# First shift's products of three quarters moved to VectorE, with one ring of eight weight buffers for the first stage

## The chip, the cores and the metric

The kernel runs on one core of a Trainium2 chip. The metric is the device time of one execution in microseconds (us). Times inside an execution come from one profiled execution and count from the start of its span. TensorE is called PE, VectorE DVE, ScalarE ACT, GpSimd POOL; DMA transfers are issued from SyncE's queue (SP).

## The reference

One transformer block on 256 tokens of width 2048, all in FP32. Its first stage is the modulation and the big input product:

```python
mod = (silu(c) @ w_ada[l] + b_ada[l])[:, None, :]
sh1, sc1, g1, sh2, sc2, g2 = split(mod, 6)
u = layer_norm(x) * (1.0 + sc1) + sh1
mix = token_mixer(u, w_in[l], ...)      # u @ w_in, sliding-window attention, gated delta rule, projections
x = layer_norm(alpha * x + g1 * mix, ...)
u = layer_norm(x) * (1.0 + sc2) + sh2
x = layer_norm(alpha * x + g2 * hier_moe(u, ...), ...)   # 32 experts, two per token
```

`sh1` and `sc1`, the first shift and the first scale, are needed before any column of `u` exists: each is a vector of 2048 numbers, and each number is a dot product of `silu(c)` with a column of 2048 weights. So 32 MB of weights are read to make them.

## The kernel before

**The first stage (0 to about 195 us).** `u` is cut into four quarters of 512 columns (four slices of 128 in `xT`, transposed). For a quarter, `first_mods` makes 512 numbers of the scale and 512 of the shift; then the quarter of `u` can be formed and multiplied. The weights of one such 512-vector are four tiles `w` of 128x2048 (1 MB each). PE takes a tile in four column-tiled matmuls into `fa` (L192, `fa<-w,crep`, named `fa` + 1 for scale or 0 for shift + quarter); after four tiles ACT copies `fa` to `fr` (L199), PE transposes it in four pieces into `fc` (L169), and DVE reduces it to the column vector (L170) and adds the bias (L171). After the shift of a quarter come, four times, DVE's modulation of an `xT` slice (L175), ACT's cast `uh` (L176, the high part of `u`) and DVE's `ul` (L177, the low part).

**The input product of a quarter.** `quarter(q)` takes five weight tiles `w_kq`, each in two half jobs: ten jobs of a quarter. A job splits its 128x1024 half tile into `wh` (ACT cast, L275) and `wl = w - wh` (DVE, L276) and then runs 24 matmuls 128x256 into PSUM `wq`: eight times the three products `uh,wh` (L280), `ul,wh` (L281), `uh,wl` (L282). Names are `wq` + quarter + tile + half. The result is copied to `a0` or `szT` by ACT in quarter 0 (L334) and added to it by DVE in quarters 1 to 3 (L336). There are three buffers for `wh`, two for `wl` and two for `wq`.

**What sets the order.** `run` writes the jobs of a quarter down and puts a step of the next quarter's modulation between them, at the pace `QCH` in steps per job: the jobs of quarter 0 run beside the modulation of quarter 1, and so on; steps left over are written after the tenth job. The order of each engine's instructions in the finished program is then set by the framework's scheduler from this code; every engine works through its own list in that order. Tiles are loaded into a pool `wp` of four buffers, the first four into two larger areas (`early_room`), all in the order in which the SP queue lists them.

**Behind it** (195 to about 400 us) the remaining columns of `u @ w_in`, the attention, the gated delta rule and the projections run, again as three matmuls for a product; the four later modulation vectors are made there on DVE (L220, 128 operations `acc<-w,csil,acc`). From about 960 us the experts' weights stream through PE.

```python
QCH = 0.73
for _ in range(8 - FM + (LT[0] >= 0)):
    next(mods)
for q in range(4):
    quarter(q, dsts)
for q in range(3):
    run(few(mods, 8), QCH, split_at=2 * TQ)
```

Of the kernel before, what the change touches and what calls it, by code (L numbers as in the profile page):

```python
# [9 lines left out]
F32 = mybir.dt.float32  # L10
# [6 lines left out]
P = 128  # L17
D = 2048
KT = D // P
S = 256  # L20
NT = S // P
# [13 lines left out]
AHEAD = ((1, 1), (1, 3), (2, 1), (2, 3), (3, 1))  # L35
LATE = 0
TQ = 5
QCH = 0.73
FM = 2
LT = (-1, 0)  # L40
GS = (2, 6, 10)
NW2 = 6
PER = (1.66, 1.55, 0.85, 2.0)
# [23 lines left out]
def tile_block(ctx: ExitStack, tc: tile.TileContext, A: dict, out: bass.AP, dbg=None, upto=99):  # L67
    nc = tc.nc
    V, SC, G, T = nc.vector, nc.scalar, nc.gpsimd, nc.tensor
    MUL, ADD, SUB = ALU.mult, ALU.add, ALU.subtract  # L70
# [4 lines left out]
    def wload(src):  # L75
        w = wp.tile([P, 2048], F32, tag="w", name="w")
        nc.sync.dma_start(w, src)
        return w
# [29 lines left out]
    ident, ones = C("ident"), C("ones")  # L108
# [21 lines left out]
    csil = rb.tile([P, KT], F32, name="csil")  # L130
    SC.activation(csil, craw[:, 0:KT], AF.Silu)
    crep = gd.tile([P, KT, 32], F32, name="crep")
# [9 lines left out]
    r2 = up.enter_context(tc.tile_pool(name="r2", bufs=1, side=R))  # L142
# [3 lines left out]
    def pg(nm):  # L146
        return ps_g.tile([P, 512], F32, tag="g", name=nm)
# [9 lines left out]
    def early_room():  # L157

        a = r1.tile([P, 1024 + 7 * 512], F32, tag="G1", name="wx0")
        b = r2.tile([P, KT, S], F32, tag="X1", name="wx1").rearrange("p k s -> p (k s)")  # L160
        return [t[:, 2048 * j:2048 * j + 2048] for t in (a, b) for j in range(2)]

    def first_mods():

        def use(i, q, mr):
            dst = (sh1c, sc1c)[i][:, 4 * q:4 * q + 4]
            p = pg(f"fc{i}{q}")
            for m in range(4):
                T.transpose(p[:, m * P:(m + 1) * P], mr[:, m * P:(m + 1) * P], ident)  # L169
            V.tensor_reduce(dst, p.rearrange("p (m j r) -> p m j r", m=4, j=4)[:, :, :, 0], axis=AX.X, op=ADD)  # L170
            V.scalar_tensor_tensor(dst, dst, float(i), craw[:, KT * (i + 1) + 4 * q:KT * (i + 1) + 4 * q + 4],  # L171
                                   op0=ADD, op1=ADD)
            if i == 0:
                for k in range(4 * q, 4 * q + 4):
                    V.tensor_scalar(xT[:, k, :], xT[:, k, :], sc1c[:, k:k + 1], sh1c[:, k:k + 1], op0=MUL, op1=ADD)  # L175
                    SC.copy(uh[:, k, :], xT[:, k, :])  # L176
                    V.tensor_tensor(ul[:, k, :], xT[:, k, :], uh[:, k, :].bitcast(F32), op=SUB)  # L177

        late = []
        room = early_room()  # L180
        for q in range(4):
            for i in (1, 0):
                pa = pg(f"fa{i}{q}")
                for t in range(4):
                    src = A["w_a01"][(4 * i + q) * 4 + t]
                    if room:
                        w = room.pop(0)
                        nc.sync.dma_start(w, src)
                    else:
                        w = wload(src)  # L190
                    for k in range(4):
                        T.matmul(pa[32 * k:32 * k + 32, :], crep[:, 4 * t + k, :], w[:, 512 * k:512 * k + 512],  # L192
                                 start=(t == 0), stop=(t == 3))
                    if late and t == LT[1 - i]:
                        use(*late.pop())
                    if t < 3:
                        yield
                mr = rb.tile([P, 512], F32, tag="mr", name=f"fr{i}{q}")
                SC.copy(mr, pa)  # L199
                if i == 0 and LT[0] < 0:  # L200
                    use(i, q, mr)
                else:
                    late.append((i, q, mr))
                yield
        if late:
            use(*late.pop())
        yield

    mrs = {}

# [39 lines left out]
    uh = r2.tile([P, KT, S], F32R, name="uh")  # L250
    ul = r2.tile([P, KT, S], F32R, name="ul")
    sh1c = gd.tile([P, KT], F32, name="sh1c")
    sc1c = gd.tile([P, KT], F32, name="sc1c")
    xT = r1.tile([P, KT, S], F32, tag="M0", name="xT")
    xx = r2.tile([P, NT, D], F32, tag="X2", name="xx")
    nc.sync.dma_start(xx[:, 0, :], A["x"][0:P, :])
    nc.sync.dma_start(xx[:, 1, :], A["x"][P:2 * P, :])
    mods = first_mods()
    for _ in range(FM):
        next(mods)  # L260
    for t in range(NT):
# [3 lines left out]
        for kq in range(4):  # L265
            p = pg(f"xt{t}{kq}")
# [5 lines left out]
    def split(w, n=1024):  # L272
        h = r1.tile([P, n], F32R, tag="wh", name="wh", bufs=3)
        lo = r1.tile([P, n], F32R, tag="wl", name="wl", bufs=2)
        SC.copy(h, w)  # L275
        V.tensor_tensor(lo, w, h.bitcast(F32), op=SUB)  # L276
        return h, lo

    def mm3(p, a, b, first, last):
        T.matmul(p, a[0], b[0], start=first, stop=False)  # L280
        T.matmul(p, a[0], b[1], start=False, stop=False)  # L281
        T.matmul(p, a[1], b[0], start=False, stop=last)  # L282
# [29 lines left out]
    def quarter(q, dsts):  # L312

        for t in range(len(dsts) // 4):
            st = {}

            def prep(hf, t=t, st=st):
                if hf == 0:
                    st["w"] = wload(A["w_kq"][q * TQ + t])
                return split(st["w"][:, hf * 1024:(hf + 1) * 1024])  # L320

            def fin(sp, hf, t=t):
                h, lo = sp
                p = ps_w.tile([P, 512], F32, tag="ws", name=f"wq{q}{t}{hf}")
                for m in range(2):
                    for k in range(4):
                        kk = slice(k * 256 + m * P, k * 256 + m * P + P)
                        mm3(p[:, m * S:(m + 1) * S], (h[:, kk], lo[:, kk]), (uh[:, 4 * q + k, :], ul[:, 4 * q + k, :]),
                            k == 0, k == 3)
                        if k % 2 and m + k < 4:  # L330
                            yield
                dst = dsts[4 * t + 2 * hf].rearrange("p m s -> p (m s)")
                if q == 0:
                    SC.copy(dst, p)  # L334
                else:
                    V.tensor_tensor(dst, dst, p, op=ADD)  # L336

            for hf in range(2):
                jobs.append((lambda hf=hf, prep=prep: prep(hf), lambda sp, hf=hf, fin=fin: fin(sp, hf)))

    def first():
        if held.get("n") is None:
            held["n"] = jobs[0][0]()

    def run(chain=None, per=1.0, adas=0.0, steps=None, drain=True, split_at=None):

        c = a = 0.0
        first()
        todo = jobs[:split_at] if split_at else list(jobs)
        for i, (_, fin) in enumerate(todo):  # L350
            cur, held["n"] = held["n"], (jobs[i + 1][0]() if i + 1 < len(jobs) else None)
            sub = fin(cur)
            for _ in range(4):
                c += per / 4
                while chain is not None and c >= 1.0:
                    c -= next(chain, None) or 1.0
                a += adas / 4
                while a >= 1.0:
                    next(steps if steps is not None else ada, None)
                    a -= 1.0  # L360
                next(sub, None)
            for _ in sub:
                pass
        del jobs[:len(todo)]
        if drain and chain is not None:
            for _ in chain:
                pass
# [379 lines left out]
    def few(it, n):  # L747
        for _ in range(n):
            next(it, None)
            yield  # L750
# [7 lines left out]
        yield  # L758

    dsts = [a0[:, i:i + 2, :] for i in range(11)] + [None] + [szT[:, i:i + 2, :] for i in range(7)] + [None]  # L760
    for _ in range(8 - FM + (LT[0] >= 0)):
        next(mods)
    for q in range(4):
        quarter(q, dsts)
    for q in range(3):
        run(few(mods, 8), QCH, split_at=2 * TQ)
    for _ in mods:
        pass
    for dst, n in ((sml, "small"), (cmx, "cmx")):
# [215 lines left out]
    for c in range(4):  # L985
        cs = slice(c * 512, (c + 1) * 512)
        uq = rw.tile([P, 4, S], F32, tag="uq", name=f"uq{c}", bufs=2)
        for t in range(NT):
            V.scalar_tensor_tensor(x[t][:, cs], x[t][:, cs], mv[:, t, 0:1], l1[0][:, cs], op0=SUB, op1=MUL)
            V.scalar_tensor_tensor(x[t][:, cs], x[t][:, cs], rs[:, t], l1[1][:, cs], op0=MUL, op1=ADD)  # L990
            p = pg(f"ut{t}{c}")
# [46 lines left out]
    def pm(nm):  # L1038
        return ps_m.tile([P, 512], F32, tag="m", name=nm)
# [46 lines left out]
    for t in range(NT):  # L1086
        p = pm(f"rk{t}")
# [441 lines left out]
```

## Time and profile before

| | |
|---|---|
| median of three runs | 1835.93 us (1833.44 to 1836.46) |
| the profiled execution | 1836.7 us, of which the span is 1834.7 us |
| PE busy | 1742.0 us (95% of the span) |
| DVE busy | 906.3 us (49%) |
| ACT busy | 516.5 us (28%) |
| mean granted clock of PE | 0.987 of full speed |
| DMA | 628.58 MB, 343 GB/s over the span |

Busy shares are means over stages with different limits. "Idle before" in a row of the trace is the time in which that engine stood still ahead of the row, with what ended it. Rows with xN join N instructions of one kind that follow each other.

### The profile page before, as it was taken

To read this page: it belongs to the slowest core of one execution; us is meant where nothing else is said; L and a number is where in the kernel's file an instruction comes from. 1 tells how busy PE (TensorE), PEld (TensorE's weight loads), DVE (VectorE), ACT (ScalarE), POOL (GpSimd) and SP (SyncE) were. 2 spreads that over 40 slices of the span, in tenths; PEclk is the share of its full clock that TensorE was granted. 3 is DMA by queue.
4 is the path that set the end of the run, shared out by engine and by line. 5 is a ranking of instruction groups with operands and counts; after the bars stand their busy time and mean duration, and the time that the engine had idled before them with its cause. 6 is when DMAs were issued, how large, how long until landed. Compare 5 with 4: busy or idle time off the path is not lost. (4 is left out here: it accounts for less than half of the span.)

```text
span 1834.7 us, 27454 instructions
## 1 busy us (share of the span) xinstructions
PE 1742.0 (95%) x11514; PEld 1122.4 (61%) x11514; DVE 906.3 (49%) x1447; ACT 516.5 (28%) x956; POOL 42.1 (2%) x47
## 2 busy tenths in 40 slices
PE   5999999999999999998899999999999999999995
PEld 3778988898999999986444443444434444344341
DVE  3355898788878878668233222332223312232135
ACT  3333699336323444434211100111101110011101
POOL 1000000102000000000000000000000000000000
PEclk8999999999999999999999999999999999999998
DMA  8888566455877578878799999999999999999995
GB/s 356 320 320 312 211 245 225 174 207 200 300 266 269 205 284 325 345 303 354 319 383 420 420 420 421 420 421 420 421 420 420 420 421 420 420 420 421 401 422 232
DMA packets 87287, 628.58 MB, mean 343 GB/s; under 512 B 9828, under 2 KB 9828, under 8 KB 11252
## 3 DMA queue, kind: packets, MB, share of 16 engines
q1 hardware_dynamic: 86832, 626.43, 85.6%
q8 instruction: 92, 1.51, 0.3%
q10 hardware_dynamic: 328, 0.36, 0.1%
q14 instruction: 35, 0.29, 0.0%
HBM read 624.65 MB, written 2.10 MB: 342 GB/s over the span
## 5 line engine op out<-in xcount | busy, mean ns | idle before, releaser
L275 ACT CAST wh<-w 128x1024 fp32r<-128x1024 f32 x216 | 225.9, 1049 | 319.0 <-PE ws L281 114.1
L276 DVE TENSOR_TENSOR wl<-w,wh 128x1024 fp32r<-128x1024 f32 x216 | 264.8, 1226 | 81.0 <-PE mx L281 22.8
L1187 PE MATMUL pg<-w,XT 128*64 128x512 f32 x1024 | 277.9, 598 | 5.0 <-DMA w<-in_w_gu 2.8
L1187 PE MATMUL pu<-w,XT 128*64 128x512 f32 x1024 | 274.6, 592 | 0.0
L280 PE MATMUL ws<-uh,wh 128*128 128x256 f32 x896 | 261.2, 292 | 1.1 <-ACT wh L275 1.1
L282 PE MATMUL ws<-uh,wl 128*128 128x256 f32 x896 | 254.5, 284 | 4.4 <-DVE wl L276 3.9
L281 PE MATMUL ws<-ul,wh 128*128 128x256 f32 x896 | 253.7, 283 | 0.0
L1225 PE MATMUL pd<-w,hT 128*64 128x512 f32 x1016 | 234.1, 599 | 0.8 <-DVE hT L1202 0.8
L1194 DVE TENSOR_TENSOR hs<-hs,pu 128x512 f32<-128x512 f32 x16 | 11.0, 688 | 429.3 <-PE pu L1187 429.3
L280 PEld LDWEIGHTS ws<-uh,wh 128*128 128x128 f32 x896 | 169.8, 190 | 11.6 <-issue 7.5
L282 PEld LDWEIGHTS ws<-uh,wl 128*128 128x128 f32 x896 | 170.1, 190 | 8.6 <-DVE wl L276 7.1
L281 PEld LDWEIGHTS ws<-ul,wh 128*128 128x128 f32 x896 | 170.1, 190 | 0.5 <-issue 0.5
L220 DVE SCALAR_TENSOR_TENSOR acc<-w,csil,acc 128x1024 f32<-128x1024 f32 x128 | 164.3, 1300 | 10.6 <-DMA w<-in_w_ada 10.3
L1187 PEld LDWEIGHTS pu<-w,XT 128*64 128x64 f32 x1024 | 77.6, 137 | 146.2 <-issue 146.2
L1187 PEld LDWEIGHTS pg<-w,XT 128*64 128x64 f32 x1024 | 72.3, 136 | 135.5 <-issue 111.8
L1166 PEld LDWEIGHTS xg<-G,xh 128*128 128x128 f32 x1024 | 118.9, 191 | 41.2 <-issue 25.8
L1225 PEld LDWEIGHTS pd<-w,hT 128*64 128x64 f32 x1016 | 66.5, 136 | 124.0 <-issue 109.6
L1166 PE MATMUL xg<-G,xh 128*128 128x128 f32 x1024 | 130.5, 281 | 6.8 <-DVE x L1242 3.5
L1193 ACT ACTIVATE hs<-pg 128x512 f32<-128x512 f32 x16 | 9.6, 598 | 439.1 <-PE pg L1187 439.1
L370 ACT CAST dh<-pd 128x512 fp32r<-128x512 f32 x64 | 37.5, 586 | 281.3 <-DVE pd L1228 160.8
L1228 DVE SCALAR_TENSOR_TENSOR pd<-pd,wsl,g2b 128x512 f32<-128x512 f32 x64 | 48.5, 758 | 104.0 <-PE pd L1225 104.0
L280 PE MATMUL wq<-uh,wh 128*128 128x256 f32 x320 | 93.7, 296 | 5.1 <-ACT uh L176 2.7
(365 smaller groups left out, 2298.0 us busy)
## 6 DMA issues: line engine op xcount, KB each, us to landing
w<-in_w_gu SPq DMA_DIRECT2D x256, 1024.0 KB, 19.8
w<-in_w_dn SPq DMA_DIRECT2D x127, 1024.0 KB, 19.8
w<-in_w_ada SPq DMA_DIRECT2D x64, 1024.0 KB, 5.0
w<-in_w_in SPq DMA_DIRECT2D x56, 1024.0 KB, 5.0
w<-in_w_a SPq DMA_DIRECT2D x28, 1024.0 KB, 6.3
w<-in_w_kq SPq DMA_DIRECT2D x20, 1024.0 KB, 6.4
w<-in_w_pab SPq DMA_DIRECT2D x16, 1024.0 KB, 5.3
w<-in_w_out SPq DMA_DIRECT2D x16, 1024.0 KB, 6.0
```

The costliest lines, as they stand in the source:

```text
L220: V.scalar_tensor_tensor(acc[:, hc], w[:, hc], csil[:, k:k + 1], acc[:, hc], op0=MUL, op1=ADD)
L275: SC.copy(h, w)
L276: V.tensor_tensor(lo, w, h.bitcast(F32), op=SUB)
L280: T.matmul(p, a[0], b[0], start=first, stop=False)
L281: T.matmul(p, a[0], b[1], start=False, stop=False)
L282: T.matmul(p, a[1], b[0], start=False, stop=last)
L370: SC.copy(h, src)
L1166: T.matmul(p[:, k * P:(k + 1) * P], xh[t][:, (4 * kq + k) * P:(4 * kq + k + 1) * P], Gs[t].bitcast(F32), start=(t == 0), stop=(t == NT - 1))
L1187: T.matmul(dst[64 * e:64 * e + 64, :], XT[:, k, 64 * e:64 * e + 64], we[:, e * 1024 + hv * 512:e * 1024 + hv * 512 + 512], start=(k == 0), ...
L1194: V.tensor_tensor(hs, hs, pup, op=MUL)
L1225: T.matmul(pd[64 * e:64 * e + 64, :], hT[:, f, 64 * e:64 * e + 64], we[:, (2 * (f % 2) + e) * 512:(2 * (f % 2) + e + 1) * 512], start=(f = ...
L1228: V.scalar_tensor_tensor(pd, pd, ws, g2b[:, cs], op0=MUL, op1=MUL)
```

## The change

For quarters 1 to 3 the products of the shift leave PE. `beside` makes them on DVE: sixteen operations 128x512 for a quarter (one `tensor_scalar`, then fifteen `scalar_tensor_tensor`, L222 and L224 of the changed kernel), each adding a quarter of a weight tile times a column of `silu(c)` to one accumulator `acc`; then four matmuls with one column (`fs`, L230) sum it over the partitions, and DVE adds the bias (L231). The scale stays on PE (`on_pe`). Both halves of a quarter's modulation now run side by side in eleven steps instead of eight, and the pace `QCH` goes from 0.73 to 1.2. From quarter 1 on all loads of the stage, those of the jobs too, go round a ring of eight buffers (`wring`): two in a tile `ms` (which also holds the accumulator), two in `xs`, four from `wp`.

```diff
-QCH = 0.73
+QCH = 1.2
+    def wring(src):
+        w = ring[turn_of[0] % len(ring)]
+        turn_of[0] += 1
+        if w is None:
+            return wload(src)
+        nc.sync.dma_start(w, src)
+        return w
...
+        def beside(q, acc, got):
+            for t in range(4):
+                for k in range(4):
+                    wk, ck = got[t][:, 512 * k:512 * k + 512], csil[:, 4 * t + k:4 * t + k + 1]
+                    if t == k == 0:
+                        V.tensor_scalar(acc, wk, ck, None, op0=MUL)
                     else:
+                        V.scalar_tensor_tensor(acc, wk, ck, acc, op0=MUL, op1=ADD)
+                    if k % 2:
                         yield
+            dst, b = column(0, q)
+            p = pg(f"fs{q}")
+            for m in range(4):
+                T.matmul(p[:, m:m + 1], acc[:, m * P:(m + 1) * P], ones[:, 0:1], start=True, stop=True)
+            V.tensor_tensor(dst, p[:, 0:4], b, op=ADD)
+            yield
...
+        ring[:] = [ms[:, 512:512 + D], ms[:, 512 + D:512 + 2 * D], xs[:, 0:D], xs[:, D:2 * D]] + [None] * 4
...
+        for q in range(1, 4):
+            got = []
+            side, main = beside(q, ms[:, 0:512], got), on_pe(1, q)
+            for n in range(11):
+                if n >= 2:
+                    next(side, None)
+                if n % 2 == 0 and n < 8:
+                    got.append(load(0, q, n // 2))
+                if n % 2 and n < 8:
+                    next(main)
+                if n == 10:
+                    modulate(q)
                 yield
...
-                    st["w"] = wload(A["w_kq"][q * TQ + t])
+                    st["w"] = wring(A["w_kq"][q * TQ + t])
...
-    for _ in range(8 - FM + (LT[0] >= 0)):
+    for _ in range(9 - FM):
...
-        run(few(mods, 8), QCH, split_at=2 * TQ)
+        run(few(mods, 11), QCH, split_at=2 * TQ)
```

Elsewhere the lines only shift: `wh` is L322, `wl` L323, the three matmuls L327 to L329, the copy L381, the add L383, `uh` L190 in the changed kernel.

The order of the program moves at three places. First ACT, quarter 0, from the cast of the fourth job on: `wh` is a job's cast, `wq<quarter><tile><half>` a job's result that is copied. Before, then after:

```order
L275 CAST wh_338<-w_299 128x1024
L334 COPY a0_196<-wq000_273 128x512
L334 COPY a0_196<-wq001_305 128x512
L275 CAST wh_376<-w_374 128x1024
L334 COPY a0_196<-wq010_342 128x512
L275 CAST wh_406<-w_374 128x1024
L334 COPY a0_196<-wq011_380 128x512
L275 CAST wh_444<-w_442 128x1024
L334 COPY a0_196<-wq020_416 128x512
L275 CAST wh_482<-w_442 128x1024
```

```order
L322 CAST wh_338<-xs_264 128x1024
L381 COPY a0_196<-wq001_306 128x512
L381 COPY a0_196<-wq010_342 128x512
L381 COPY a0_196<-wq011_378 128x512
L322 CAST wh_374<-w_372 128x1024
L322 CAST wh_412<-w_372 128x1024
L381 COPY a0_196<-wq020_420 128x512
L381 COPY a0_196<-wq021_458 128x512
L322 CAST wh_447<-ms_263 128x1024
L322 CAST wh_487<-ms_263 128x1024
```

Before, a cast and a copy alternate, and the cast of job 5 stands ahead of the copy of job 3 (`wq011`). After, both casts of jobs 4 and 5 (`wh_374`, `wh_412`) stand behind the copies of jobs 2 and 3, and both casts of jobs 6 and 7 behind the copies of jobs 4 and 5.

Second ACT at the end of quarter 0, where quarter 1 of `u` is formed: `fr` is the copy of the last `fa`, `uh` the cast of the new quarter's slices. Before, then after:

```order
L275 CAST wh_596<-w_594 128x1024
L275 CAST wh_659<-w_594 128x1024
L334 COPY szT_197<-wq041_600 128x512
L199 COPY fr01_638<-fa01_505 128x512
L176 CAST uh_100<-xT_104 128x256
L275 CAST wh_691<-w_689 128x1024
L176 CAST uh_100<-xT_104 128x256 x3
```

```order
L381 COPY szT_197<-wq030_491 128x512
L381 COPY szT_197<-wq031_539 128x512
L213 COPY fr11_511<-fa11_319 128x512
L190 CAST uh_100<-xT_104 128x256
L322 CAST wh_535<-w_533 128x1024
L322 CAST wh_567<-w_533 128x1024
L190 CAST uh_100<-xT_104 128x256 x3
L322 CAST wh_601<-w_599 128x1024
```

Before, all ten jobs of quarter 0 are cast and run ahead of `fr`, and `wh_691`, behind the first `uh`, belongs to quarter 1. After, jobs 8 and 9 of quarter 0 (`wh_535`, `wh_567`, results `wq040`, `wq041`) stand behind `fr` and behind the first `uh`; PE's list has the same turn:

```order
L208 MATMUL fa11_319<-xs_264,crep_82 32x512 x4
L183 MATMUL fc11_513<-cst_61,fr11_511 128x128 x4
L230 MATMUL fs1_605<-cst_61,ms_263 128x1 x4
L327 MATMUL wq040_571<-uh_100,wh_535 128x256
L328 MATMUL wq040_571<-ul_101,wh_535 128x256
L327 MATMUL wq041_623<-uh_100,wh_567 128x256
L328 MATMUL wq041_623<-ul_101,wh_567 128x256
L329 MATMUL wq040_571<-uh_100,wl_536 128x256
```

So PE has the last scale tile, the transposes, the four summing matmuls and then at once job 8. The ends of quarters 1 and 2 read the same way.

Third DVE in the middle of quarter 1, from the add of job 3 (`wq111`) on; `wl` is a job's low part. Before, then after:

```order
L336 TENSOR_TENSOR a0_196<-a0_196,wq111_770 128x512
L276 TENSOR_TENSOR wl_797<-w_764,wh_796 128x1024
L336 TENSOR_TENSOR a0_196<-a0_196,wq120_806 128x512
L276 TENSOR_TENSOR wl_835<-w_832,wh_834 128x1024
L336 TENSOR_TENSOR a0_196<-a0_196,wq121_838 128x512
L276 TENSOR_TENSOR wl_873<-w_832,wh_872 128x1024
```

```order
L383 TENSOR_TENSOR a0_196<-a0_196,wq110_723 128x512
L224 SCALAR_TENSOR_TENSOR ms_263<-ms_263,csil_80 128x512 x2
L323 TENSOR_TENSOR wl_754<-xs_264,wh_753 128x1024
L383 TENSOR_TENSOR a0_196<-a0_196,wq111_757 128x512
L323 TENSOR_TENSOR wl_791<-xs_264,wh_790 128x1024
L383 TENSOR_TENSOR a0_196<-a0_196,wq120_798 128x512
L224 SCALAR_TENSOR_TENSOR ms_263<-w_796,csil_80,ms_263 128x512 x3
L383 TENSOR_TENSOR a0_196<-a0_196,wq121_838 128x512
L224 SCALAR_TENSOR_TENSOR ms_263<-w_796,csil_80,ms_263 128x512
L323 TENSOR_TENSOR wl_827<-w_824,wh_826 128x1024
L323 TENSOR_TENSOR wl_869<-w_824,wh_868 128x1024
```

Before, the `wl` of job j+2 follows the add of job j. After, two products stand between the add of job 2 (`wq110`) and the `wl` of job 4 (`wl_754`), and the `wl` of job 6 (`wl_827`) stands behind the add of job 5 (`wq121`), with a product between. Quarter 2 reads the same way.

## Rows read from the trace of the kernel before

**Rows 1.** The profile page: the span, the busy time of each engine, and the GB/s that the DMA moved in 40 equal slices of the span (four of them and a quarter are the first stage).

```profile
span 1834.7 us, 27454 instructions
PE 1742.0 (95%) x11514; PEld 1122.4 (61%) x11514; DVE 906.3 (49%) x1447; ACT 516.5 (28%) x956; POOL 42.1 (2%) x47
...
GB/s 356 320 320 312 211 245 225 174 207 200 300 266 269 205 284 325 345 303 354 319 383 420 420 420 421 420 421 420 421 420 420 420 421 420 420 420 421 401 422 232
```

**Rows 2.** A stretch of the first stage: length, then busy time and number of instructions of PE, PEld, DVE, ACT, POOL, then granted clock, DMA share and GB/s.

```profile
140.00:160.00 20.00, 20.00 (x165) 16.73 (x168) 9.51 (x13) 7.12 (x7) 0.00 (x0) 1.00 0.91 340
```

**Rows 3.** What PE waited for longest between 34 and 200 us: us in total, times, longest.

```profile
PE wq L280 <- ACT uh L176: 2.7, 2, 1.4
PE wq L280 <- ACT wh L275: 2.4, 1, 2.4
```

**Rows 4.** The timeline of PE where it waits for the first tiles.

```profile
26.99 1.06 PE L192 MATMUL fa<-w,crep 128*32 128x512 f32 x8 [1.43 <-DMA w<-in_w_a]
29.46 1.06 PE L192 MATMUL fa<-w,crep 128*32 128x512 f32 x8 [1.41 <-DMA w<-in_w_a]
```

**Rows 5.** The timeline of PE around a scale or shift tile in the middle of a quarter.

```profile
42.26 0.28 PE L280 MATMUL wq<-uh,wh 128*128 128x256 f32 x1
42.47 1.06 PE L192 MATMUL fa<-w,crep 128*32 128x512 f32 x8
43.47 0.38 PE L281 MATMUL wq<-ul,wh 128*128 128x256 f32 x1
```

**Rows 6.** PE's `wq` matmuls in quarter 1 from the first at full pace to the end of its last `fa`: length, busy time and number, clock, DMA share, GB/s.

```profile
82.75:119.16 36.41, 28.52 (x226) 1.00 0.86 320
```

**Rows 7.** The timeline of PE at the transposes of a scale in mid-quarter, and at two pieces of four matmuls with few columns each.

```profile
63.50 0.66 PE L169 MATMUL fc<-cst,fr 128*128 128x128 f32 x4
63.91 0.36 PE L281 MATMUL wq<-ul,wh 128*128 128x256 f32 x1
...
213.76 0.59 PE L430 MATMUL cl<-cum,cmx 128*128 128x8 f32 x4
214.21 0.37 PE L428 MATMUL cl<-cum,cmx 128*128 128x8 f32 x2
```

**Rows 8.** The timeline of all engines at the end of quarter 0.

```profile
74.48 1.92 PE L192 MATMUL fa<-w,crep 128*32 128x512 f32 x16
76.47 0.59 ACT L199 COPY fr<-fa 128x512 f32<-128x512 f32 x1 [1.30 <-PE fa L192]
77.11 0.66 PE L169 MATMUL fc<-cst,fr 128*128 128x128 f32 x4 [0.71 <-ACT fr L199]
78.21 1.06 DVE L175 TENSOR_SCALAR xT<-xT,sc1c,sh1c 128x256 f32<-128x256 f32 x3
78.66 0.41 ACT L176 CAST uh<-xT 128x256 fp32r<-128x256 f32 x1 [1.60 <-DVE xT L175]
79.11 0.69 PE L280 MATMUL wq<-uh,wh 128*128 128x256 f32 x2 [1.35 <-ACT uh L176]
80.04 0.41 PE L282 MATMUL wq<-uh,wl 128*128 128x256 f32 x1
...
82.75 0.28 PE L280 MATMUL wq<-uh,wh 128*128 128x256 f32 x1
```

**Rows 9.** The timeline of PE at the ends of quarter 1 and of quarter 2.

```profile
118.10 1.06 PE L192 MATMUL fa<-w,crep 128*32 128x512 f32 x8
123.97 0.42 PE L282 MATMUL wq<-uh,wl 128*128 128x256 f32 x1
...
163.88 1.48 PE L387 MATMUL ba<-xT,sml 128*32 128x256 f32 x18
```

**Rows 10.** Stretches of 2 us behind waits of PE (columns as in rows 2): the ends of quarters 0, 1 and 2, and a single wait of 2.03 us at 292.6.

```profile
80.00:82.00 2.00, 2.00 (x11) 2.00 (x11) 1.10 (x3) 0.93 (x4) 0.00 (x0) 0.50 0.97 410
...
124.00:126.00 2.00, 2.00 (x11) 2.00 (x11) 0.21 (x1) 0.00 (x0) 0.00 (x0) 0.50 1.02 430
...
164.00:166.00 2.00, 2.00 (x28) 0.97 (x25) 1.93 (x7) 1.16 (x4) 0.00 (x0) 1.00 0.99 414
...
292.00:294.00 2.00, 0.57 (x6) 0.33 (x4) 0.74 (x4) 1.95 (x7) 0.00 (x0) 1.00 1.03 406
294.00:296.00 2.00, 1.30 (x9) 1.08 (x10) 1.98 (x3) 1.98 (x6) 0.00 (x0) 1.00 0.95 356
```

**Rows 11.** The timeline of ACT: two casts in a row, and a copy with a cast in quarter 0.

```profile
35.43 1.99 ACT L275 CAST wh<-w 128x1024 fp32r<-128x1024 f32 x2
...
49.46 0.59 ACT L334 COPY a<-wq 128x512 f32<-128x512 f32 x1 [2.50 <-PE wq L282]
49.95 1.05 ACT L275 CAST wh<-w 128x1024 fp32r<-128x1024 f32 x1
```

**Rows 12.** The timeline of DVE: an add and a low part in quarter 2, and two products 128x512 of which the second needs the first.

```profile
135.39 0.69 DVE L336 TENSOR_TENSOR a<-a,wq 128x512 f32<-128x512 f32 x1 [2.21 <-PE wq L282]
136.00 1.22 DVE L276 TENSOR_TENSOR wl<-w,wh 128x1024 fp32r<-128x1024 f32 x1
...
1829.40 0.75 DVE L127 SCALAR_TENSOR_TENSOR x<-x,mvd,l 128x512 f32<-128x512 f32 x1
1830.18 0.75 DVE L128 SCALAR_TENSOR_TENSOR x<-x,rsd,l 128x512 f32<-128x512 f32 x1
```

**Rows 13.** What PE waited for longest between 200 and 420 us.

```profile
PE py L544 <- DVE G L535: 4.0, 1, 4.0
```

More of the change, by code (lines that the diff above doesn't have):

```diff
@@ L161, in early_room, with column, turn @@
         return [t[:, 2048 * j:2048 * j + 2048] for t in (a, b) for j in range(2)]
+    ring, turn_of = [None], [0]
+    def wring(src):
[5 more added lines that the diff above has]
+        return w
     def first_mods():
-        def use(i, q, mr):
-            dst = (sh1c, sc1c)[i][:, 4 * q:4 * q + 4]
+        def column(i, q):
+            return (sh1c, sc1c)[i][:, 4 * q:4 * q + 4], craw[:, KT * (i + 1) + 4 * q:KT * (i + 1) + 4 * q + 4]
+        def turn(i, q, mr):
+            dst, b = column(i, q)
             p = pg(f"fc{i}{q}")
@@ L170, in use @@
             V.tensor_reduce(dst, p.rearrange("p (m j r) -> p m j r", m=4, j=4)[:, :, :, 0], axis=AX.X, op=ADD)
[L171 to L177, printed above, removed]
@@ L179, in first_mods @@
-        late = []
-        room = early_room()
[L181 to L188, printed above, removed]
-                    else:
[L190 to L196, printed above, removed]
-                        yield
[L198 to L203, printed above, removed]
+            V.scalar_tensor_tensor(dst, dst, float(i), b, op0=ADD, op1=ADD)
@@ new lines, in modulate, with load @@
+        def modulate(q):
+            for k in range(4 * q, 4 * q + 4):
+                V.tensor_scalar(xT[:, k, :], xT[:, k, :], sc1c[:, k:k + 1], sh1c[:, k:k + 1], op0=MUL, op1=ADD)
+                SC.copy(uh[:, k, :], xT[:, k, :])
+                V.tensor_tensor(ul[:, k, :], xT[:, k, :], uh[:, k, :].bitcast(F32), op=SUB)
+        room = early_room()
+        def load(i, q, t):
+            src = A["w_a01"][(4 * i + q) * 4 + t]
+            if room:
+                w = room.pop(0)
+                nc.sync.dma_start(w, src)
+                return w
+            return wring(src)
@@ new lines, in on_pe @@
+        def on_pe(i, q):
+            pa = pg(f"fa{i}{q}")
+            for t in range(4):
+                w = load(i, q, t)
+                for k in range(4):
+                    T.matmul(pa[32 * k:32 * k + 32, :], crep[:, 4 * t + k, :], w[:, 512 * k:512 * k + 512],
+                             start=(t == 0), stop=(t == 3))
+                if t < 3:
+                    yield
+            mr = rb.tile([P, 512], F32, tag="mr", name=f"fr{i}{q}")
+            SC.copy(mr, pa)
+            turn(i, q, mr)
+            yield
@@ new lines, in beside @@
+        def beside(q, acc, got):
+            for t in range(4):
+                for k in range(4):
+                    wk, ck = got[t][:, 512 * k:512 * k + 512], csil[:, 4 * t + k:4 * t + k + 1]
+                    if t == k == 0:
+                        V.tensor_scalar(acc, wk, ck, None, op0=MUL)
+                    else:
+                        V.scalar_tensor_tensor(acc, wk, ck, acc, op0=MUL, op1=ADD)
+                    if k % 2:
+                        yield
+            dst, b = column(0, q)
[3 more added lines that the diff above has]
+            V.tensor_tensor(dst, p[:, 0:4], b, op=ADD)
+            yield
@@ new lines, in first_mods @@
+        yield from on_pe(1, 0)
+        yield from on_pe(0, 0)
+        modulate(0)
+        ms = r1.tile([P, 1024 + 7 * 512], F32, tag="G1", name="ms")
+        xs = r2.tile([P, NT, D], F32, tag="X2", name="xs").rearrange("p t d -> p (t d)")
+        ring[:] = [ms[:, 512:512 + D], ms[:, 512 + D:512 + 2 * D], xs[:, 0:D], xs[:, D:2 * D]] + [None] * 4
+        turn_of[0] = 0
+        yield
+        for q in range(1, 4):
[10 more added lines that the diff above has]
+                    modulate(q)
@@ L204, in first_mods @@
                 yield
-        if late:
-            use(*late.pop())
-        yield
     mrs = {}
```

1 line of the change is left out of this document (removed).

## The prediction

> **What bounds the kernel now.** I read the page first: PE is busy 1742 of 1834.7 us [rows 1], so whatever PE saves or loses counts, unless a wait takes its place. Then the table of stretches: in the first stage PE is busy without a gap (20.00 of 20.00 us) at full clock, while the DMA stands at 0.91 with 340 GB/s and reaches 420 GB/s later in the run [rows 2, 1]. Then PE's waits from 34 to 200 us: they lead to ACT's `uh` and `wh`, 5.1 us together, and none to a DMA [rows 3]; only before 34 us does PE wait for tiles, which then land 2.47 us apart [rows 4]. So this stage is PE's own work, in order, plus the chain at each quarter's end.
>
> **What the change removes.** Twelve shift tiles leave PE. In the timeline a tile takes the place of one matmul from 42.26 to 43.47, 1.21 us against a pace of 0.118 (24 matmuls, a job, are 2.84 us): 1.09 us [rows 5]. Averaged, quarter 1 runs from 82.75 to 119.16, 36.41 us, with 226 `wq` matmuls [rows 6] (26.7 us), one set of transposes (63.50 to 63.91, about 0.5 us with what follows [rows 7]) and eight tiles: 9.2 us, 1.15 each. I take 1.15: 13.8 us. Of two sets of transposes in a quarter one goes, in mid-quarter, 3 x 0.5 = 1.5 us. Gain 15.3 us.
>
> **What it adds to PE.** Four one-column matmuls per quarter. The trace has none; the nearest are `cl`, four records 128x8 (two matmuls, as `fa` has eight records for four) from 213.76 to 214.21, 0.22 us a matmul [rows 7]: 0.9 us for four. The lower bound is the transposes' 0.5. I take 0.9, in all 2.7 us.
>
> **The products on DVE.** One of 0.75 us starts 0.78 us behind the one that it needs [rows 12], so sixteen are 12.5 us of a quarter. Ten adds (0.61 start to start) and ten low parts (1.22) are 18.3 us; together 31 of the 43.9 us between two quarters' ends (80.04 to 123.97 [rows 8, 9]). DVE has the room, so by share they cost nothing. They cost where they stand ahead of something PE waits for.
>
> **Loads.** The stage still reads 13 tiles for a quarter, 32 us at 2.47 each [rows 4] against 43 us, and the ring holds eight tiles. I cost the ring at nothing: PE's work hides the loads, and without that cover a quarter could not fall under 32 us.
>
> **Stalls from ACT's order, quarter 0.** The casts of jobs 4 and 5 now stand behind the copy of job 3, which needs job 3's end, E. In the timeline a copy starts about 0.2 us behind the last matmul (74.39 to 74.59 at the quarter's end) and the cast 0.49 us behind the copy (49.46, 49.95); a cast is 1.05, two in a row 1.99 us [rows 11]. So the cast of job 4 ends at E+1.74, its `wl` (1.22 us [rows 12]) at about E+3.0. PE in that time has four matmuls (0.47 us) whose operands are ready. It loses 2.6 us; the same for jobs 6 and 7 behind job 5's copy: 5.2 us. Before, these casts were two jobs ahead.
>
> **Stalls from DVE's order, quarters 1 and 2.** The `wl` of job 4 is ready behind job 2's end by the start, the add, two products and itself: 0.2 + 0.61 + 2 x 0.78 + 1.22 = 3.6 us; PE has job 3 (2.84) and two ready matmuls (0.24) until it needs it: 0.5 us lost (nothing, if a scale tile falls in between). The `wl` of job 6 now follows the add of job 5, which needs job 5's end, and one product: 0.2 + 0.61 + 0.78 + 1.22 = 2.8 us, less four ready matmuls: 2.3 us. That is 2.8 us a quarter, 5.6 us in all; without the first place it is 4.6.
>
> **The quarters' ends.** Before, the chain from the end of the last `fa` (76.40) ran through `fr` (76.47), `fc` (77.11), DVE (78.21) and `uh` (78.66) to the first smooth matmul at 80.04 [rows 8]: 3.64 us, of which PE worked 0.8, so 2.83 lost. Then matmuls start 0.21 us apart until 82.75 [rows 8], and the granted clock is 0.50, the 1.2 GHz level [rows 10]: 13 matmuls x 0.1 = 1.3 us more. The second end (119.16 to 123.97 [rows 9]) by the same reading: 3.3 lost and 1.5 for the clock. At the third, eighteen records of `ba` fill the gap [rows 9] and the clock stays 1.00 [rows 10]: 1.05 us lost. Together 10 us.
> After: jobs 8 and 9 stand behind the turn, and their casts behind the first `uh`. From the end of `fa`: `fr` 0.07 to 0.66, transposes to 1.4, `fs` to 2.3, DVE's add and modulation, `uh` to 3.1; then the cast of job 8 (3.4 to 4.4), its `wl` to 5.7. Inside PE has 0.5 + 0.9 + 0.5 us of work, so it loses 3.85 us, and by the two ends before about 1.75 more at the low clock: 5.6 us. The third end has no `ba` in the gap now (it stands some 300 matmuls later). So 3 x 5.6 = 16.8 against 10: 6.7 us lost (0.9 of `fs` is counted above; without low clock at any end it would be 1.5).
>
> **The low clock behind the new stalls.** The four stalls of 2.3 and 2.6 us lie between the single wait of 2.03 us, after which the clock stayed at 1.00, and the end of quarter 0 with 2.83 us lost, after which it was 0.50 [rows 10]. So each costs nothing or about 1.45 us, 0 to 5.8 in all. I take half, 2.9.
> The Trainium skill's page "TensorE: Matmul & The Clock Gate", section "A second HAM failure mode: psum-queue depth-cycling", says that frequent micro-idles between groups of matmuls are enough to make the clock swing, with a cost at each return. By it all four would cost their 1.45 us. No run here shows such short stalls in a row.
>
> **The sum.** -15.3 + 2.7 + 5.2 + 5.6 + 6.7 + 2.9 = +7.8 us. Against the profiled execution, 1836.7 us (a span of 1834.7 and 2.0 around it), that is 1844.5. The median shown is 0.8 lower: **1843.7 us**. The second stage I leave as it is: its order moves as well, and its largest single wait is 4.0 us, before `py` [rows 13]; I bound it by 3 us either way.
>
> **The rivals.**
> *The stalls don't reach PE (faster).* The removed work stands, the quarters' ends cost as worked out, but the casts and low parts come in time, because PE finds enough ready matmuls at each place: -15.3 + 2.7 + 6.7 = -5.9 us, 1830. For it: before, PE's waits for `wh` and `uh` are three in all [rows 3], so the framework's order has served PE well in mid-quarter. Against: the copy of job 3 can't start before job 3 is over, and `wq` has two buffers. The point from which it decides: stalls at the four `wh` and `wl` places under 1.5 us each (5.9 / 4).
> *The load is the hidden bound (faster).* If tiles late in a small pool held the stage back, eight buffers would give quarters of 32 us in place of 43: about -30 us, 1806. Against it stands that PE waits for no DMA there [rows 3].
> *The second stage gives it back (same).* The 4.0 us before `py` [rows 13] and some 3 us of low clock behind it vanish, because later work now precedes `py`: +7.8 - 7 = +0.8 us, 1836.7. For it: the scheduler places the second stage anew. Against: the chain to `py` runs over DVE and keeps its length, so only the cover changes.
> *Every new stall drops the clock (slower).* All four places cost their 1.45 us, 5.8 us in place of 2.9, and the two of 0.5 us, which the sum gave none, too: 8.7 in all, +13.6 us, 1849.5. The page named above speaks for it; the wait of 2.03 us without a drop speaks against it [rows 10].
> *The change does not free PE.* Twelve tiles gone from PE are in the program's order, so this can only be by the stalls above; it has no case of its own.
>
> **How the numbers follow.** My case (the sum; without low clock behind the stalls 1841, with it all but 1847) has 0.48, every stall with its low clock 0.12, the second stage giving back 0.20, the stalls not reaching PE 0.17, the loads 0.03. What a measurement of this kernel can tell from no change is about 0.2%, 3.7 us; that makes slower 0.60, same 0.20, faster 0.20. The range leaves out the loads, half of the case without stalls, and a little at the top: 1830 to 1852.
>
> **What would show it.** In the changed kernel's first stage: behind 34 us twelve scale tiles (96 records of L208, eight a tile) stand where 24 tiles of L192 stood. PE should wait for `wh` (L322) about 2.6 us twice between 50 and 65 us; for `wl` (L323) 2 to 3 us in each of the two next quarters; and for `fr`, `uh` and `wh` near 4 us at each of the three ends, the third as long as the others, with a granted clock of 0.50 behind them. The stage should end about 8 us later than before. If PE's waits for `wl` and `wh` away from the ends stay under 2 us in all, the step on the order is wrong and the kernel is faster; if a wait on a DMA appears on `fa` or the products, the step on the loads is wrong.

## The result, and the profile after

The changed kernel takes 1845.69 us (median of five, 1843.61 to 1846.81) against 1835.58 us for the kernel before: a ratio of 1.0056 with a 95% interval of 1.0041 to 1.0071. It is 10.1 us slower; 7.8 were forecast. Its profiled execution, 1843.6 us, lies 2 us under its median, and that of before 1 us above its own, so the two traces stand only 7.1 us apart.

The page of the changed kernel, the lines that answer to [rows 1]:

```profile
span 1841.8 us, 27343 instructions
PE 1735.6 (94%) x11430; PEld 1124.1 (61%) x11430; DVE 938.6 (51%) x1492; ACT 514.5 (28%) x953; POOL 43.4 (2%) x47
```

PE is busy for 6.4 us less and DVE for 32.3 us more, but the span is 7.1 us longer: PE stands still. Its waits from 34 to 210 us, the whole list (us in total, times, longest), against 5.1 us for ACT's casts in [rows 3]:

```profile
PE wq L327 <- ACT wh L322: 14.3, 11, 2.4
PE wq L329 <- DVE wl L323: 4.2, 5, 1.2
PE fc L183 <- ACT fr L213: 2.1, 3, 0.7
PE wq L327 <- DVE a L383: 1.3, 2, 0.6
```

No DMA stands there. The places are the ones named. First the cast of job 4 behind the copy of job 3 in quarter 0 (timeline of ACT, DVE and PE):

```profile
50.49 0.28 PE L329 MATMUL wq<-uh,wl 128*128 128x256 f32 x1
50.81 0.59 ACT L381 COPY a<-wq 128x512 f32<-128x512 f32 x1 [2.25 <-PE wq L329]
51.29 1.99 ACT L322 CAST wh<-w 128x1024 fp32r<-128x1024 f32 x2
52.39 0.39 PE L327 MATMUL wq<-uh,wh 128*128 128x256 f32 x1 [1.62 <-ACT wh L322]
53.34 0.58 PE L327 MATMUL wq<-uh,wh 128*128 128x256 f32 x1 [0.44 <-ACT wh L322]
53.71 0.42 PE L328 MATMUL wq<-ul,wh 128*128 128x256 f32 x1
```

Job 3 ends at 50.61 (50.49 and one pace), and PE is smooth again from 53.71, 3.1 us later, with three matmuls in between (52.39, 52.62 and 53.34): 2.7 us lost, 2.6 forecast. The same two waits return at 63.35 and 64.30, and 2.6 us are lost there.

Second, the low part of job 6 behind the add of job 5 in quarter 1 (timeline of DVE and PE; the first row is the last matmul of job 5, which ends one pace later, at 104.78):

```profile
104.66 0.28 PE L329 MATMUL wq<-uh,wl 128*128 128x256 f32 x1
104.98 0.69 DVE L383 TENSOR_TENSOR a<-a,wq 128x512 f32<-128x512 f32 x1
105.59 0.75 DVE L224 SCALAR_TENSOR_TENSOR ms<-w,csil,ms 128x512 f32<-128x512 f32 x1
105.82 0.36 PE L327 MATMUL wq<-uh,wh 128*128 128x256 f32 x1 [0.65 <-DVE a L383]
106.25 2.35 DVE L323 TENSOR_TENSOR wl<-w,wh 128x1024 fp32r<-128x1024 f32 x2
107.52 0.39 PE L329 MATMUL wq<-uh,wl 128*128 128x256 f32 x1 [1.23 <-DVE wl L323]
107.75 0.28 PE L327 MATMUL wq<-uh,wh 128*128 128x256 f32 x1
```

After the add, the product and the low part, the matmul that needs it starts at 107.52, 2.74 us behind the end of job 5. Four matmuls run in between: two of job 6 (104.78 and 104.90), and two of job 7 (105.82 and 106.01), which wait 0.65 us for the add first. With their 0.47 us taken off, 2.3 us are lost, as forecast. Quarter 2 has the same waits at 150.22 and 151.92. Third, the end of quarter 0, which answers to [rows 8]:

```profile
71.20 1.06 PE L208 MATMUL fa<-xs,crep 128*32 128x512 f32 x8
72.33 0.59 ACT L213 COPY fr<-fa 128x512 f32<-128x512 f32 x1 [0.44 <-PE fa L208]
72.97 0.66 PE L183 MATMUL fc<-cst,fr 128*128 128x128 f32 x4 [0.71 <-ACT fr L213]
73.47 0.95 PE L230 MATMUL fs<-cst,ms 128*128 128x1 f32 x8
75.17 0.41 ACT L190 CAST uh<-xT 128x256 fp32r<-128x256 f32 x1 [2.25 <-DVE xT L189]
75.48 1.99 ACT L322 CAST wh<-w 128x1024 fp32r<-128x1024 f32 x2
76.58 0.39 PE L327 MATMUL wq<-uh,wh 128*128 128x256 f32 x1 [2.16 <-ACT wh L322]
77.52 0.58 PE L327 MATMUL wq<-uh,wh 128*128 128x256 f32 x1 [0.45 <-ACT wh L322]
```

From the end of `fa` (72.26) through `fr`, `fc`, `fs`, `uh` and the two casts of jobs 8 and 9 it is 5.64 us to the smooth start at 77.90 (5.7 forecast). The ends of quarters 1 and 2 show the same three waits, 0.71, 2.16 and 0.45, at 117, 121 and 122 and at 162, 165 and 166 us, and the same 5.64 us.

Last, the granted clock (2 us each; columns as in [rows 2]):

```profile
54.00:56.00 2.00, 2.00 (x13) 1.75 (x16) 1.97 (x3) 0.00 (x0) 0.00 (x0) 0.50 1.01 422
64.00:66.00 2.00, 1.71 (x14) 1.46 (x18) 2.00 (x3) 0.24 (x1) 0.00 (x0) 1.00 1.01 422
78.00:80.00 2.00, 2.00 (x11) 2.00 (x11) 1.92 (x4) 1.34 (x3) 0.00 (x0) 0.50 0.50 115
108.00:110.00 2.00, 2.00 (x11) 1.19 (x13) 0.60 (x1) 0.00 (x0) 0.00 (x0) 0.50 0.97 360
154.00:156.00 2.00, 2.00 (x11) 0.50 (x4) 0.00 (x0) 0.00 (x0) 0.00 (x0) 0.57 1.02 426
166.00:168.00 2.00, 1.64 (x7) 1.64 (x8) 2.00 (x3) 2.00 (x5) 0.00 (x0) 0.50 1.01 426
```

Behind three of the four mid-quarter stalls and behind all three ends (the one near 122 is not shown) the clock falls to its 1.2 GHz level; behind the second stall of quarter 0 (64 to 66) it stays at full speed. That is six falls where the kernel before has two [rows 10].

Three marks of the traces of all kernels, read from PE's rows (start of the last `wq` matmul, and start of the first `xg`, the first of the later stages that all kernels share), with the median of the runs and the ratio to the kernel before with its interval:

| kernel | last `wq` | first `xg` | span | median | ratio |
|---|---|---|---|---|---|
| before | 194.6 | 875.9 | 1834.7 | 1835.6 | |
| changed | 201.5 | 883.0 | 1841.8 | 1845.7 | 1.0056 (1.0041 to 1.0071) |
| ring_alone | 192.9 | 877.4 | 1838.2 | 1839.9 | 1.0015 (1.0006 to 1.0024) |
| act_in_order | 194.4 | 877.1 | 1837.5 | 1838.2 | 1.0009 (1.0000 to 1.0018) |
| dve_in_order | 200.2 | 878.5 | 1837.7 | 1842.7 | 1.0039 (1.0026 to 1.0051) |
| both_in_order | 196.6 | 877.4 | 1838.3 | 1838.8 | 1.0014 (1.0006 to 1.0023) |
| vector_early | 183.6 | 864.6 | 1825.6 | 1827.7 | 0.9955 (0.9941 to 0.9968) |
| tensor_early | 194.8 | 874.1 | 1834.1 | 1837.0 | 1.0006 (0.9997 to 1.0015) |
| vector_early_few_products | 177.7 | 861.5 | 1821.6 | 1823.1 | 0.9920 (0.9905 to 0.9934) |
| vector_early_ring_of_4 | 210.4 | 891.5 | 1851.4 | 1856.2 | 1.0110 (1.0095 to 1.0126) |
| vector_late_reduce | 179.9 | 859.5 | 1820.3 | 1821.2 | 0.9923 (0.9905 to 0.9940) |

Two things limit the first column. The first `wq` matmul starts anywhere from 34.0 to 35.6 us in these eleven traces (34.65 before, 35.62 changed), so 1 us between two marks says little. And the 32 records of `ba`, a small product that takes 1.93 us by itself, stand inside the stage in some traces and behind its last `wq` in others: all of them behind it in the changed kernel and in act_in_order, 26 of 32 inside it in the kernel before and in ring_alone, 18 in vector_early_few_products, all inside it in the other runs.

### The profile page after: what moved, and what is told of

Read it like the earlier page. It is cut to its first block, busy times and chain, and to the rows that moved or that the text cites. A ratio compares the mean times of both kernels' runs of the same rounds, so it can differ in the third digit from the quotient of the medians.

```text
span 1841.8 us, 27343 instructions
## 1 busy us (share of the span) xinstructions
PE 1735.6 (94%) x11430; PEld 1124.1 (61%) x11430; DVE 938.6 (51%) x1492; ACT 514.5 (28%) x953; POOL 43.4 (2%) x47
## 5 line engine op out<-in xcount | busy, mean ns | idle before, releaser
L322 ACT CAST wh<-w 128x1024 fp32r<-128x1024 f32 x194 | 202.9, 1050 | 273.4 <-PE ws L328 116.4
L323 DVE TENSOR_TENSOR wl<-w,wh 128x1024 fp32r<-128x1024 f32 x194 | 238.2, 1230 | 70.4 <-PE mx L328 22.8
L327 PE MATMUL ws<-uh,wh 128*128 128x256 f32 x896 | 261.1, 291 | 2.6 <-ACT wh L322 2.6
L329 PE MATMUL ws<-uh,wl 128*128 128x256 f32 x896 | 254.1, 284 | 3.3 <-DVE wl L323 3.1
L327 PEld LDWEIGHTS ws<-uh,wh 128*128 128x128 f32 x896 | 169.6, 189 | 13.5 <-issue 7.5
L329 PEld LDWEIGHTS ws<-uh,wl 128*128 128x128 f32 x896 | 169.7, 189 | 7.1 <-DVE wl L323 5.3
L327 PE MATMUL wq<-uh,wh 128*128 128x256 f32 x320 | 95.4, 298 | 15.6 <-ACT wh L322 14.3
## 6 DMA issues: line engine op xcount, KB each, us to landing
w<-in_w_a SPq DMA_DIRECT2D x15, 1024.0 KB, 12.6
```

## The experiments

The theory: TensorE's saved work is real, and the order of ScalarE's and VectorE's lists, at three kinds of place, takes it back and more. The rivals: the ring does it; VectorE's time does it; the order does not decide.

**ring_alone.** The kernel before with the ring:

```diff
-                        w = wload(src)
+                        w = wring(src)
...
-                    st["w"] = wload(A["w_kq"][q * TQ + t])
+                    st["w"] = wring(A["w_kq"][q * TQ + t])
```

> The kernel before, with nothing but the ring of eight buffers for the first stage's loads; all shift products stay on TensorE, and TensorE's order in the stage is word for word that of before. Theory (the change loses by the order of ScalarE's and VectorE's lists at quarter ends and in mid-quarter, and by the low clock behind it): the ring costs and gives nothing, 1835.6 us within 2. Rival (the loss is in the ring: other addresses, tiles that arrive later): a good part of the 10 us that the changed kernel is slower, 1840 us or more.

1839.9 us, 4.2 us above the kernel before and so not within the 2 us of the theory; by the number alone the rival could stand. PE's list in the stage is that of before, and its waits are those of [rows 3], place by place:

```profile
PE wq L296 <- ACT uh L187: 2.7, 2, 1.4
PE wq L296 <- ACT wh L291: 2.4, 1, 2.4
```

The stage even ends 1.7 us earlier, mostly because the clock falls behind one quarter's end (at 122 to 126 us) and not behind two. But from there to `xg` it takes 684.5 us against 681.3, where the framework placed the second stage anew, and from `xg` to the end 2 us more than before. Each of these two stretches has a fall of the clock that the kernel before does not have there (0.50 from 296 to 298 us, and 0.52 to 0.62 from 1705 to 1709 us); what else makes them longer is open. So the ring by itself brings nothing and costs some 4 us, none of it in the first stage. In the changed kernel this cost does not appear: from the last `wq` to `xg` it takes 681.5 us, and from `xg` to the end as long as before (958.8 us).

**act_in_order, dve_in_order, both_in_order.** The three quarters' jobs are written so that the split of job j+2 follows the end of job j, and one or both engines issue what stands there in the order in which it is written:

```diff
-    for q in range(3):
-        run(few(mods, 11), QCH, split_at=2 * TQ)
+    with tc.manual_schedule(engines={mybir.EngineType.Activation, mybir.EngineType.DVE}):
+        for q in range(3):
+            run(few(mods, 11), QCH, split_at=2 * TQ, deep=True)
...
             for _ in sub:
                 pass
+            if deep and i + 2 < len(jobs):
+                ready.append(jobs[i + 2][0]())
```

> The changed kernel with ScalarE alone held to an order written out for the first stage: the cast of job j+2 stands right behind the copy of job j, and every cast of a quarter stands ahead of the turn to the next. VectorE's and TensorE's lists stay the framework's. Theory: both stalls of quarter 0 go (2 x 2.06 us idle and about 1.4 us at the low clock behind the first), and the end of quarter 0 shrinks from 3.3 us idle and 1.4 us low clock to the 0.7 us for the transposes; VectorE's stalls in quarters 1 and 2 stay. 1845.7 - 5.5 - 4.0 = 1836 us. Rival (the order does not decide): 1845 us within 3.

1838.2 us: 7.5 us of the 10 come back with ScalarE's order alone (9.5 expected). Both stalls of quarter 0 are gone and job 8 starts right behind `fs`; what is left at each end is, beside the 0.7 us for the transposes, a wait of 1.9 to 2.4 us for `wl`. PE's two longest rows from 34 to 210 us, where the changed kernel had 14.3 us in eleven waits for `wh` (the one that is left stands at the start of the stage):

```profile
PE wq L329 <- DVE wl L323: 9.7, 8, 2.4
PE wq L327 <- ACT wh L322: 2.4, 1, 2.4
```

> The changed kernel with VectorE alone held to an order written out for the first stage: the low part of job j+2 stands right behind the add of job j, then the products of that job. ScalarE's list stays the framework's. Theory: in quarters 1 and 2 the waits for the low parts go (2 x 2.5 us idle and 2 x 1.4 us low clock), and their ends shrink by about 4 us each, while quarter 0 stays as in the changed kernel: 1845.7 - 7.8 - 8 = 1830 us. Rival (the order does not decide): 1845 us within 3. Rival (only ScalarE's order matters): 1842 us or more.

1842.7 us, a miss by 13, and within the rival that only ScalarE's order matters (1842 or more). The mid-quarter waits of quarters 1 and 2 are gone as expected. But the ends did not shrink by 4 us each; both_in_order shows why. So what VectorE's order in mid-quarter costs is read from the trace of the changed kernel alone; no run shows it as a time.

> The changed kernel with ScalarE and VectorE both held to the written order of the two runs above. Theory: all mid-quarter waits go and what stays is 0.7 us for the transposes and some 2 us of modulation at each quarter's end: 1845.7 - 5.5 - 7.8 - 3 x 3 = 1823 us. Rival (the order does not decide): 1845 us within 3. If the products' share of VectorE's time were the bound, TensorE would still wait for low parts in quarters 1 and 2, and the time would stay above 1833 us.

1838.8 us, a miss by 16 and no better than ScalarE alone. No wait in mid-quarter is left. The end of quarter 0 (timeline of ACT, DVE and PE):

```profile
75.55 0.41 ACT L190 CAST uh<-xT 128x256 fp32r<-128x256 f32 x1 [1.82 <-DVE xT L189]
75.98 0.43 DVE L191 TENSOR_TENSOR ul<-xT,uh 128x256 fp32r<-128x256 f32 x1 [0.47 <-ACT uh L190]
76.33 0.41 DVE L189 TENSOR_SCALAR xT<-xT,sc1c,sh1c 128x256 f32<-128x256 f32 x1
77.23 0.38 PE L327 MATMUL wq<-uh,wh 128*128 128x256 f32 x1 [0.26 <-ACT uh L190]
78.45 0.38 PE L327 MATMUL wq<-uh,wh 128*128 128x256 f32 x1 [0.26 <-ACT uh L190]
```

As written, DVE modulates one slice, waits for its cast, makes its low part and only then begins the next: 1.22 us a slice, while PE needs 0.35 for the three matmuls of one. The framework's order has three modulations in a row [rows 8]. My written order mended the middle of the quarters and spoilt their ends, about 3 us each for the four slices. Such a wait by steps hardly shows among PE's waits (1.7 us for `uh` in all); the starts of the matmuls show it.

**vector_early and tensor_early.** Both engines in written order, the slices modulated before the first low part, and the turn earlier; the second does the same to the kernel before, with the products on TensorE:

```diff
-QCH = 1.2
+QCH = 1.3
...
                 SC.copy(uh[:, k, :], xT[:, k, :])
+            for k in range(4 * q, 4 * q + 4):
                 V.tensor_tensor(ul[:, k, :], xT[:, k, :], uh[:, k, :].bitcast(F32), op=SUB)
```

> The changed kernel with ScalarE and VectorE held to the written order as in both_in_order, and the turn to the next quarter earlier: the pace is 1.3 steps a job instead of 1.2, and the four slices are modulated and cast before the first low part. The last sum is then written 34 matmuls ahead of the next quarter, and the transposes have six matmuls of a job ahead of them. Theory (what both_in_order still lost is the quarters' ends, some 7 us each): they shrink to about 1 us, the first stage ends near 175 us instead of 196.6, and the time is 1838.8 - 3 x 6.5 = 1819 us. Rival (TensorE's saved work is taken back elsewhere): 1836 us within 4.

1827.7 us, 8.3 us faster than the kernel before, though 8.7 us slower than expected. From 42 us to the end of the stage the clock does not fall. PE still waits (from 33 to 200 us; 2.4 and 0.5 of it at the very start):

```profile
PE wq L330 <- DVE wl L324: 4.4, 6, 1.8
PE wq L328 <- DVE szT L384: 3.3, 2, 1.7
PE wq L328 <- ACT wh L323: 2.4, 1, 2.4
```

> The kernel before, all shift products on TensorE and no ring, with the same written order of ScalarE and VectorE and an early turn (pace 0.9 steps a job instead of 0.73). Theory: only the quarters' ends change, 10 us lost before and some 2 to 3 us now, so 1835.6 - 7 = 1828.5 us, and the difference to vector_early is the work that the change takes from TensorE, 12.6 us by the prediction's terms. Rival (the products on VectorE bring nothing even where the order is no obstacle): the same time as vector_early within 3 us.

1837.0 us, no faster than before (7 expected). It waits 2.2 and 2.4 us at the ends of quarters 0 and 1, with a clock fall behind the second, where the add stands behind the eight steps of the modulation (118.41 to 121.05) in DVE's written order:

```profile
79.43 0.39 PE L281 MATMUL wq<-uh,wh 128*128 128x256 f32 x1 [2.21 <-ACT wh L276]
121.87 0.36 PE L281 MATMUL wq<-uh,wh 128*128 128x256 f32 x1 [2.37 <-DVE szT L337]
```

With written orders of the same kind on both sides the pair is 9.3 us apart, and 11.2 us at the last `wq`, against 12.6 for the work that leaves PE by the prediction's terms. The pair is not a clean price of that work: behind the start of the stage tensor_early still waits 6.4 us and has the clock fall, vector_early waits 7.2 us at other places. And tensor_early was not carried further, so what the best order would bring the kernel before is not shown.

**vector_early_few_products.** Fourteen of sixteen products left out:

```diff
-                    else:
+                    elif t == 3 and k == 3:
                         V.scalar_tensor_tensor(acc, wk, ck, acc, op0=MUL, op1=ADD)
```

> vector_early with 14 of the 16 products of each quarter's shift left out on VectorE (the first and the last stay), so the shift of three quarters is not the reference's; loads, ring and all else stay. Theory (VectorE has room for them): the same time as vector_early within 2 us. Rival (VectorE's share bounds the stage once its order is right): 5 us or more faster than vector_early.

1823.1 us, 4.6 us faster than vector_early, and the intervals do not overlap: near the rival's mark of 5. (The shift of three quarters is then not the reference's.) PE's waits for low parts fall from 4.4 to 2.4 us and for adds from 3.3 to 0.9. So the products are not free beside a quarter that has shrunk from 43.9 us to 38.4 (76.61 to 115.02, where in vector_early the matmuls of quarters 1 and 2 become smooth): the 31 us of the prediction and 3 us of modulation leave 4 us for any standstill. Whether VectorE is full there, or stands still at the wrong place, this run does not tell; vector_late_reduce does.

**vector_early_ring_of_4.** The four pool buffers alone:

```diff
-        ring[:] = [ms[:, 512:512 + D], ms[:, 512 + D:512 + 2 * D], xs[:, 0:D], xs[:, D:2 * D]] + [None] * 4
+        ring[:] = [None] * 4
```

> vector_early with the four pool buffers alone in place of the ring of eight. A quarter still loads 13 tiles, 32 us at 2.47 us each, and has 34 to 35 us of TensorE's work. Theory (with the stalls gone the loads come close to the bound, and the ring is what covers them): TensorE and VectorE wait for tiles in quarters 1 to 3, and the time is 5 to 20 us above vector_early. Rival (four buffers are enough, the ring costs nothing and gives nothing): the same as vector_early within 2 us.

1856.2 us, 28.4 us slower, more than expected. The waits of PE and, below, of ACT from 33 to 200 us:

```profile
PE wq L327 <- ACT wh L322: 11.4, 5, 2.6
PE wq L329 <- DVE wl L323: 7.6, 12, 1.8
PE fa L209 <- DMA w<-in_w_a: 3.0, 3, 1.1
...
ACT wh L322 <- DMA w<-in_w_kq: 39.8, 6, 11.7
```

For PE the DMA is named for 3.0 us only; but the casts that it waits for are late because ACT waits 39.8 us for their tiles (6.2 in vector_early). The DMA is not full meanwhile, its share is 0.78 from 34 to 75 us against 0.94 in vector_early: with nothing changed but the buffers, the loads wait for them. The ring is what hides the loads here.

**vector_late_reduce.** vector_early's list stands still at the transposes (timeline of DVE, quarter 1): the scale's reduction, written right behind them, holds products and an add that were ready.

```profile
103.67 0.17 DVE L184 TENSOR_REDUCE sc1c<-fc 128x4 f32<-128x16 f32 x1 [2.80 <-PE fc L183]
103.96 1.53 DVE L225 SCALAR_TENSOR_TENSOR ms<-w,csil,ms 128x512 f32<-128x512 f32 x2
105.41 0.68 DVE L384 TENSOR_TENSOR szT<-szT,wq 128x512 f32<-128x512 f32 x1
```

The edit moves the reduction into the modulation's step and the low parts of `u` one step on:

```diff
+            while turned:
+                turned.pop()()
             for k in range(4 * q, 4 * q + 4):
...
+            if q:
+                yield
+            for k in range(4 * q, 4 * q + 4):
                 V.tensor_tensor(ul[:, k, :], xT[:, k, :], uh[:, k, :].bitcast(F32), op=SUB)
```

> vector_early, with the scale's reduction and bias moved on VectorE from right behind the transposes to the modulation step, and the four low parts of u written one step behind the casts. Theory (vector_early still loses 7.2 us in seven waits for low parts and adds, since VectorE's list stands still 7.7 us on the transposes): these waits shrink by 4 to 6 us, and the time is 1827.7 - 5 = 1822.5 us, near the run with few products. Rival (VectorE is simply full in these quarters): 1827 us within 2.

1821.2 us, 6.5 us faster than vector_early, with all products in place. So the rival that VectorE is simply full (1827 us) does not hold: the time came back by the order alone. How much of it is the standstill at the transposes, and how much the later low parts of `u`, which the same edit moves, no run separates. PE from 33 to 200 us:

```profile
PE wq L339 <- ACT wh L334: 3.9, 2, 2.4
PE wq L341 <- DVE wl L335: 2.6, 5, 0.8
PE wq L340 <- DVE ul L199: 1.2, 1, 1.2
```

The waits for adds are gone. This version beats both kernels: a ratio of 0.9923 to the one before, with an interval of 0.9905 to 0.9940, some 15 us, and 14.7 us of them are there at the last `wq` (179.9 against 194.6).

## Why the prediction was right, step by step

- **The work taken off PE** (15.3 us less 2.7 for `fs`): behind 34 us 96 records of `fa` stand where 192 stood, as foreseen. The pair vector_early and tensor_early shows 11.2 us at the last `wq` and 9.3 in the medians, with different waits in the two, so the gain is there and its size is known to a few us only. `fs` took 0.82 to 0.85 us from its first matmul to the next one in the written orders, where nothing waits in between; 0.9 was taken.
- **ACT's order, quarter 0**: 2.7 and 2.6 us at the two places, 2.6 taken (its own terms, 3.0 less 0.47, give 2.5). act_in_order, which undoes it and the casts behind the turn, gets back 7.5 us.
- **DVE's order, quarters 1 and 2**: 2.3 us measured at job 6 (2.3 taken), and a wait of 0.64 at job 4 (0.5 taken), in both quarters alike.
- **The quarters' ends**: 5.64 us from `fa` to smooth, 5.7 taken, at all three, the third too without `ba`; each with a clock fall.
- **The low clock**: three of four stalls had a fall, half was taken: 1.5 us more than the sum has.
- **Sum**: the last `wq` starts 6.9 us later. All of `ba` now runs behind the stage (32 records, 1.93 us from 203.16), where before 26 of the 32 stood inside, so like for like the stage is 8.5 us longer, against 7.8 in the sum. The second stage gave 1.4 us back; its wait before `py` is 3.2 us instead of 4.0 [rows 13]. The mechanism is confirmed place by place; that the sum comes out within 1 us is partly luck, since the two traces already differ by 1.0 us at the first `wq`, the low clock had one fall more than taken, and the medians are 10.1 us apart where the traces are 7.1.
- **The step on the loads** ("I cost the ring at nothing") is right for the time of this change and wrong as a thought: the ring of four shows that the ring is what makes the faster versions possible.
- **"DVE has the room, so by share they cost nothing"** held for the busy share and not for the order. In vector_early 4.6 us lay in the products, and vector_late_reduce got 6.5 us back with every product in place, by moving what stood ahead of them.

Of the rivals, the stalls did reach PE; the second stage gave back 1.4 of the 7 us that rival needed; the loads were no bound in the kernel before (ring_alone's first stage gains 1.7 us, most of it the clock, where 30 us were at stake); and the clock fell behind most, not all, of the stalls.

## What to carry to other kernels

When work moves to an engine with free time, look at what its list does in between, not at its busy share: an instruction that stands one place too late behind a wait costs the bound engine the whole chain, here 2.3 to 2.7 us four times over, and 5.6 us from the last tile to smooth matmuls at each turn. Compare the order of the lists before and after, price each place from durations in the trace, and then repair the order before judging the idea: the same change was 10 us slower than the kernel before with the framework's order and some 15 us faster than it with a written one. A written order has to be looked at as closely as the framework's: dve_in_order and both_in_order fell short by 13 and 16 us, and their traces show the low parts of `u` written too early, one slice at a time.

## What the runs showed of the hardware that I had not expected

The length of a wait alone does not decide whether PE's clock falls. In the changed kernel the same pair of waits (1.62 and 0.44 us) was followed by a granted clock of 0.50 at 54 us and by 1.00 at 64 us. In ring_alone the waits at the ends of quarters 0 and 1 are those of the kernel before, yet only one of the two was followed by a fall, which is where most of its 1.7 us came from. In vector_early waits of 1.65 and 0.57 us within 3 us leave the clock at full speed (104 to 108 us, granted clock, DMA share and GB/s in the last three columns):

```profile
104.00:106.00 2.00, 0.58 (x5) 0.38 (x4) 1.97 (x4) 0.82 (x1) 0.00 (x0) 1.00 1.03 426
106.00:108.00 2.00, 1.20 (x8) 1.02 (x9) 1.97 (x4) 0.00 (x0) 0.00 (x0) 1.00 1.00 422
```

The Trainium skill's page "TensorE: Matmul & The Clock Gate", section "A second HAM failure mode: psum-queue depth-cycling", tells of a bf16 kernel in which TensorE's short and frequent idle times between groups of matmuls make the clock swing. Most stalls of the changed kernel go with that, though they are few and its matmuls are FP32; vector_early's, of the same size, do not. What tells the two apart is not shown here; a sum can only carry such a fall as a chance.
